# A two-layer decoder trunk on one core: products of 512 columns read their moving tile from two halves in turns

## The chip, the core and the metric

The kernel runs on one core of a Trainium2 chip, as one launch. The time is the device time of that core in microseconds. The kernel before took 1157.42 us, the median of three runs (1157.29, 1157.42 and 1157.46 us). A core has an engine for matrix products (PE, with a separate track PEld for loading the stationary operand), two elementwise engines (DVE and ACT), a third one (POOL), a queue engine (SP), and 16 DMA engines.

## The reference

A batch of one sequence of 512 tokens with 1024 features passes through two layers. Layer 0 mixes tokens with a convolution module, layer 1 with sparse attention. Each mixer is followed by a SwiGLU block. Cut to what is multiplied:

```python
D_MODEL, SEQ, DEPTH, D_FF = 1024, 512, 2, 2816
def swiglu_ffn(h, w_in, w_out):
    gate, up = jnp.split(h @ w_in, 2, axis=-1)
    return (jax.nn.silu(gate) * up) @ w_out
# layer 0:  h = rmsnorm(x, g);  x += silu(layernorm(causal_depthwise_conv(glu(h @ w_in)))) @ w_out
# layer 1:  h = rmsnorm(x, g);  q, k, v, gates = split(h @ w_in);  x += (gated compressed + selected + window attention) @ w_out
# both:     h = rmsnorm(x, g);  x += swiglu_ffn(h, w_in, w_out)
```

Everything is float32. The kernel takes each float32 operand apart into a high part, rounded to the type float32r, and a low part, the rest, also float32r, and adds three products: high times high, high times low, low times high.

## The kernel before, in words

**Layout.** Features lie on the 128 partitions, tokens along the free axis. The residual stream is eight tiles `x[0..7]` of 128 features by 512 tokens. A product of 512 columns loads a 128 by 128 block of weights as the stationary operand and reads a tile of 128 by 512 tokens as the moving one; it writes one bank of PSUM with 512 float32 columns, one per token.

**The products of 512 columns.** `mm3` (lines 320 to 323) issues the three products of one block: `wh` with `xh`, `wh` with `xl`, `wl` with `xh`. It is called from `proj_start` (line 395; the first four output tiles of a projection, k by k, with the first k written out by hand), `proj_tile` (line 424; one output tile, 8 k-steps, 24 products), `reg_tile` in the SwiGLU block (line 1117), the loop over 12 output tiles in the attention projections (line 1814) and `row_mm` (line 1191; 14 rows of the second SwiGLU matrix, each with 8 output tiles). The convolution's start (lines 499 to 513) writes its products out by hand. In the profile these products are named `pp<-hh,wh`, `pp<-hl,wh`, `pp<-a,wh`, `pp<-oh,wh`, `st<-row,wh`, `st<-ah,wh` and so on: output, then the moving tile and the weights.

**Other products.** The rest of both SwiGLU blocks goes through `product` (line 1013): block products of 256 columns (`st<-ball,sh`, `st<-ball,wh`), whose moving operand is `ball`. The attention's value projections (`v_mm`, line 1844) use slices of `hh` and `hl` as the stationary operand and 304 or 256 columns of weights as the moving one. Scores, transposes, value products and sums of squares have shapes of their own.

**Who writes the moving tiles.** `split_x` (line 347) makes `hh` and `hl` from `x`: ACT scales and rounds into `hh`, DVE writes scaled `x` minus `hh` into `hl`. It serves the convolution's input, both SwiGLU inputs and the attention's input (the columns `V_NM0`, `V_NF0`, `V_NF1`, `V_NM1` of the gains); `split_last` (line 884) does the same for the eighth tile of a SwiGLU block. `ln_mul` and `ln_low` (lines 808 to 820) make the tile `a` of the convolution's output projection, in two ACT activations and a DVE subtraction. `divide` (line 895) and `row_part` (line 1159) take the SwiGLU products `ys` apart for the row stage. `out_parts` (line 2019) makes `oh` and `ol` from the attention's output.

**Who reads the results.** In the attention, `gain` and `square` (lines 1489 and 1505) copy a projection tile out of PSUM on ACT, `v_cmp` (line 1764) multiplies two others into the tile `kr` on DVE, and lines 2137 to 2146 add the output projection to `x` on DVE. The SwiGLU and convolution stages multiply or add the PSUM tile on DVE.

**Order.** Weights arrive through a list `units` in program order: `w_dma` loads a 128 by 1024 tile on SP's queue, `w_hi` rounds it on ACT, `w_lo` subtracts on DVE, `next_w` (line 271) hands it over and starts the one after. Many instructions are pinned to program order (`held`, `pe`, `order`, `hold`), and the hooks of `proj_start`, the tables `BESIDE`, `V_BESIDE` and `FILL` and the dictionaries `ROW_AT`, `RAW_AT`, `SUM_AT` say beside which product each elementwise step is issued. The rest is ordered by the framework's scheduler. Each instruction is recorded at line 153, the helper that passes it on, so the profile is read by tile names.

Of the kernel before, what the change touches and what calls it, by code (L numbers as in the profile page):

```python
# [14 lines left out]
AF = mybir.ActivationFunctionType  # L15
ALU = mybir.AluOpType
# [3 lines left out]
P = 128  # L20
T = 512
D = 1024
NK = 8
# [12 lines left out]
V_NM0, V_NF0, V_NM1, V_NF1 = 0, 8, 16, 24  # L36
# [129 lines left out]
def trunk(ctx: ExitStack, tc: tile.TileContext, A, out):  # L166
# [71 lines left out]
    def held(ins):  # L238
        return tc.keep_in_program_order(ins) if hold[0] else ins
# [69 lines left out]
    def v(col, n=1):  # L309
        return vec[:, col:col + n]  # L310
# [6 lines left out]
    nc.gpsimd.memset(halfpi, math.pi / 2)  # L317


    def mm3(ps, wh, wl, xh, xl, first, last):  # L320
        held(nc.tensor.matmul(ps, wh, xh, start=first, stop=False))
        held(nc.tensor.matmul(ps, wh, xl, start=False, stop=False))
        held(nc.tensor.matmul(ps, wl, xh, start=False, stop=last))

    def rsqrt(pool, a, rows, n, tag):

# [20 lines left out]
    def split_x(m, gcol):  # L347
        hh[m] = hps[0].tile([P, T], F32R, tag=f"hh{m}", name=nm(f"hh{m}"))
        hl[m] = hps[0].tile([P, T], F32R, tag=f"hl{m}", name=nm(f"hl{m}"))
        g = v(gcol + m)  # L350
        held(nc.scalar.activation(hh[m], x[m], AF.Copy, scale=g))
        held(nc.vector.scalar_tensor_tensor(hl[m], x[m], g, hh[m], ALU.mult, ALU.subtract))

    def sum_x(m, acc, eng=None, on_v=False):
        sq = acc if m == 0 else tp.tile([P, T], F32, tag="sq", name=nm("sq"))
# [39 lines left out]
    def proj_start(pool, tag, xh, xl, hooks=None, pre=None, into=None):  # L395

        hooks = hooks or {}
        pss = [] if into is None else into
        pss.extend(pool.tile([P, T], F32, tag=tag, name=nm("pp")) for _ in range(4))
        if pre:  # L400
            pre(0)
        for i in range(4):
            wh, wl = next_w()
            for k2 in range(2):
                k = 2 * i + k2
                if pre and k + 1 < NK:
                    pre(k + 1)
                if k == 0 and pre:
                    for w, z in ((wh, xh), (wl, xh), (wh, xl)):
                        for m in range(4):  # L410
                            held(nc.tensor.matmul(pss[m], w[:, m * P:(m + 1) * P], z[0], start=w is wh and z is xh,
                                                  stop=False))
                for m in range(4 if k or not pre else 0):
                    c = slice(k2 * T + m * P, k2 * T + (m + 1) * P)
                    mm3(pss[m], wh[:, c], wl[:, c], xh[k], xl[k], k == 0, k == NK - 1)
                    if (k, m) in hooks:
                        hooks[k, m]()
                if k2 == 0:
                    w_lo()
                if k in hooks:  # L420
                    hooks[k]()
        return pss
# [15 lines left out]
    def conv_module():  # L438
        acc = new_acc()
        with ExitStack() as cx:  # L440
# [53 lines left out]
            for k in range(NK):  # L494
                if k < NK - 1:
                    split_x(k, V_NM0)
                if k == NK - 2:
                    split_x(NK - 1, V_NM0)
                if k == 0:
                    wh, wl = first_w()  # L500
                elif k % 2 == 0:
                    wh, wl = next_w(False)
                if k == 0:
                    load_tables()
                    for w, z in ((wh, hh), (wl, hh), (wh, hl)):
                        for m in range(2):
                            held(nc.tensor.matmul(pend[m], w[:, m * P:(m + 1) * P], z[0], start=w is wh and z is hh,
                                                  stop=False))
                    continue
                for m in range(2):  # L510
                    c = slice(k % 2 * 256 + m * P, k % 2 * 256 + (m + 1) * P)
                    for w, z in ((wh, hh), (wl, hh), (wh, hl)):
                        held(nc.tensor.matmul(pend[m], w[:, c], z[k], start=False, stop=z is hl and k == NK - 1))
            for k in range(NK):
                if k == 3:
                    w_hi(state["next"])
# [291 lines left out]
            def ln_mul(i):  # L808
                pe(nc.vector.tensor_tensor(vch[i], vch[i], rs, ALU.mult))
                lny[i] = ct.tile([P, T], F32, tag="A", bufs=3, name=f"lny{i}")  # L810
                if i == 0:
                    box["a"] = [cp.tile([P, NK * T + A_ASIDE], F32R, tag="bd", bufs=BAND_BUFS, name=f"a{s}")
                                [:, A_ASIDE:].rearrange("p (k t) -> p k t", k=NK) for s in range(2)]
                ah.append(box["a"][0][:, i, :])
                for z in (ah[i], lny[i]):
                    pe(nc.scalar.activation(z, vch[i], AF.Silu, scale=v(V_LNG + i), bias=v(V_LNB + i)))

            def ln_low(i):
                al.append(box["a"][1][:, i, :])
# [30 lines left out]
    def ffn(acc, gnext, layer, between=None):  # L850
# [9 lines left out]
        def pe(ins):  # L860
            return ins if order[0] else tc.keep_in_program_order(ins)

        with ExitStack() as cx:
# [20 lines left out]
            def split_last(part):  # L884
                m, g = NK - 1, v(gcol + NK - 1)
                if part == 0:
                    hh[m] = hps[0].tile([P, T], F32R, tag=f"hh{m}", name=nm(f"hh{m}"))
                    hl[m] = hps[0].tile([P, T], F32R, tag=f"hl{m}", name=nm(f"hl{m}"))
                    nc.scalar.activation(hh[m], x[m], AF.Copy, scale=g)
                else:  # L890
                    nc.vector.scalar_tensor_tensor(hl[m], x[m], g, hh[m], ALU.mult, ALU.subtract)

            ah, al, ys = {}, {}, {}

            def divide(f, pool):
                ah[f] = pool.tile([P, T], F32R, tag=f"ah{f}", name=nm("ah"))
                al[f] = pool.tile([P, T], F32R, tag=f"al{f}", name=nm("al"))
                held(nc.scalar.activation(ah[f], ys[f], AF.Copy))
                held(nc.vector.tensor_tensor(al[f], ys[f], ah[f], ALU.subtract))

            def new_y(f):
                k = f - EARLY - 1
# [256 lines left out]
            def row_part(f):  # L1159
                if f in ROW_SLOT:  # L1160
                    t = sw.tile([P, 2 * T], F32R, tag=ROW_SLOT[f], name=nm("row"))
                    rh[f] = h_, l_ = t[:, :T], t[:, T:]
                else:
                    rh[f] = h_, l_ = [sw.tile([P, T], F32R, tag="gc" + e, name=nm("row")) for e in "hl"]
                pe(nc.scalar.activation(h_, ys[f], AF.Copy))
                pe(nc.vector.tensor_tensor(l_, ys[f], h_, ALU.subtract))

            def block(c, d, e, neg=False):
                h_, l_ = bh[c][:, d], bl[c][:, d]
# [194 lines left out]
    def nsa(acc, cosT, sinT, gnext):  # L1364
# [124 lines left out]
        def gain(e, ps):  # L1489

            if e < 2:
                q = ap_.tile([P, T], F32, tag=f"kr{e}", name=nm("kraw"))
            elif e < 6:
                q = tp.tile([P, T], F32, tag=("sq", "sq", "acc", "Rb")[e - 2], name=nm("kraw"), bufs=2 if e < 4 else 1)
            else:
                q = op.tile([P, T], F32, tag=f"o{e - 6}", name=nm("qraw"))
            (ks if e < 6 else oT).append(q)
            raw.append(q)
            nc.scalar.activation(q, ps, AF.Copy, scale=v(V_KG + e // 2 if e < 6 else V_QG))
            rot = rots[e] = C["rots"][e % 2]  # L1500
            for b in (0, 64):
                nc.sync.dma_start(rot[b:b + 8], q[b + 8:b + 16])
                nc.sync.dma_start(rot[b + 8:b + 16], q[b:b + 8])

        def square(e, ps):
            sqs[e] = (qk.tile([P, T], F32, tag="q2", name=nm("qsq"), bufs=Q2B) if e in (4, 5) else
                      kp.tile([P, T], F32, tag="qsq", name=nm("qsq"), bufs=SQB))
            nc.scalar.activation(sqs[e], ps, AF.Square)

        def first_out():  # L1510
            gain(0, firsts[0])
# [26 lines left out]
        def to_cmp(c, a):  # L1538
            return kr[c][:, :, a, :].rearrange("p q n -> p n q")
# [10 lines left out]
        def seq16(t):  # L1550
            return t.rearrange("p (n q) -> p n q", q=16)
# [124 lines left out]
        def pe(ins):  # L1676
            return ins if order[0] else tc.keep_in_program_order(ins)
# [85 lines left out]

        def v_cmp():
            for a in range(2):
                nc.vector.tensor_tensor(to_cmp(1, a), seq16(pss[2 + a]), seq16(R), ALU.mult)
            cmp_move(1)

        extra["vc"] = v_cmp
# [364 lines left out]
        with ExitStack() as cxo:  # L2134
            po = pool(cxo, "apo", 8, space=PSUM, **rw)
            acc = new_acc()
            for m in range(NK):
                ps = proj_tile(po, "po", oh, ol)
                pin.clear()
                order[0] = m == NK - 1  # L2140
                nc.vector.tensor_tensor(x[m], x[m], ps, ALU.add)
                if m < NK - 1:
                    finish_x(m, gnext, acc, fin(m))
                else:
                    sum_x(m, acc, fin(m))
                order[0] = False
# [184 lines left out]
```

## Time and profile before

| | |
|---|---|
| median of three runs | 1157.42 us |
| profiled execution, first to last instruction (span) | 1156.3 us |
| outside the span, from these two | 1.1 us |
| granted TensorE clock, mean | 1.000 |
| PE busy | 1151.0 us, 8341 products |
| PEld busy | 1011.6 us, 8341 loads |
| DVE busy | 867.4 us, 1558 instructions |
| ACT busy | 585.1 us, 1118 instructions |
| POOL busy | 402.6 us, 441 instructions |
| DMA | 164.27 MB, mean 142 GB/s |

Busy time of PE is the union of modelled durations: the end of a product is modelled, and neighbours overlap in the record. How long a product really keeps PE is read from the distance between the starts of neighbours. A group's row gives, behind the bar, the busy time and the mean duration of one, and then the idle time of the engine ahead of it.

### The profile page before, as it was taken

The page shows a single profiled execution, that of the slowest core. Times are in us where ns is not written, and L with a number is a line of the kernel's source. Part 1 is how long each engine was busy: PE and PEld are TensorE (multiplying, and loading weights), DVE is VectorE, ACT ScalarE, POOL GpSimd, SP SyncE. Part 2 cuts the span into 40 slices and gives each one's busy share as a digit, 9 for nine tenths or more (in the row PEclk, how much of TensorE's full clock was granted, in tenths as well). Part 3 has the DMA queues.
Part 4 walks back from the last instruction along what each step waited for, and adds up shares of the span by engine and source line. Part 5 has one row for each costly group of instructions (what it writes and reads, how often), then busy time and mean ns, then how long its engine had stood idle before and what let it go on. Part 6 is the DMA issues. An engine that isn't in the chain of part 4 may idle for free.

```text
span 1156.3 us, 21728 instructions
## 1 busy us (share of the span) xinstructions
PE 1151.0 (100%) x8341; PEld 1011.6 (87%) x8341; DVE 867.4 (75%) x1558; ACT 585.1 (51%) x1118; POOL 402.6 (35%) x441
## 2 busy tenths in 40 slices
PE   9999999999999999999999999999999999999998
PEld 7888788899999988998778877778889999998898
DVE  7898786998777568875676778764699877756566
ACT  6312464565555444454333688763455555544443
POOL 1029122054444101333233577752304444430031
PEclk9999999999999999999999999999999999999999
DMA  9744428278777532534364232112736877762352
GB/s 372 268 124 125 98 91 218 92 195 200 198 192 192 155 119 92 153 104 106 110 160 113 63 75 55 38 38 91 200 109 162 205 198 190 194 184 92 109 128 73
DMA packets 86552, 164.27 MB, mean 142 GB/s; under 512 B 36656, under 2 KB 37808, under 8 KB 85680
## 3 DMA queue, kind: packets, MB, share of 16 engines
q1 hardware_dynamic: 66800, 108.48, 30.9%
q0 software_dynamic: 19504, 54.37, 20.1%
q8 instruction: 65, 1.06, 0.4%
q14 instruction: 39, 0.32, 0.1%
q10 hardware_dynamic: 144, 0.04, 0.0%
HBM read 147.23 MB, written 5.28 MB: 132 GB/s over the span
## 4 chain that ended last, share of the span: by engine, by line
PE 96%; DVE 2%; issue 1%; DMA 1%; ACT 0%; SPq 0%; DVEq 0%; ACTq 0%
PE st L153 50%; PE pp L153 29%; PE O L153 4%; PE S L153 3%; PE T L153 3%; PE pv L153 2%; PE cpe L153 1%; DVE cv L153 1%; PE warm L153 1%; PE psc L153 1%; DVE u L153 0%; DMA swap<-u 0%; PE z L153 0%; PE psq L153 0%; PE rbc L153 0%
## 5 line engine op out<-in xcount | busy, mean ns | idle before, releaser
L153 PE MATMUL st<-ball,sh 128*128 128x256 f32 x1760 | 304.9, 276 | 0.0
L153 PEld LDWEIGHTS st<-ball,sh 128*128 128x128 f32 x1760 | 265.4, 188 | 1.3 <-ACT c L153 1.0
L153 PE MATMUL st<-ball,sl 128*128 128x256 f32 x880 | 242.5, 276 | 0.0
L153 DVE TENSOR_TENSOR wl<-wr,wh 128x1024 fp32r<-128x1024 f32 (+4 forms) x145 | 179.9, 1240 | 83.3 <-ACT wh L153 83.2
L153 ACT ACTIVATE wh<-wr 128x1024 fp32r<-128x1024 f32 (+4 forms) x144 | 148.6, 1032 | 169.0 <-PE st L153 60.2
L153 POOL DMA_DIRECT2D S<-fw_x x88 | 78.3, 890 | 277.0 <-DVE sl L153 221.2
L153 POOL TENSOR_TENSOR S<-S,wr 128x512 f32<-128x512 f32 x84 | 118.2, 1407 | 147.6 <-DMA wr<-fw_op 119.3
L153 PEld LDWEIGHTS st<-ball,sl 128*128 128x128 f32 x880 | 165.3, 188 | 0.0
L153 PE MATMUL pp<-hh,wh 128*128 128x512 f32 x384 | 153.2, 399 | 0.1
L153 PE MATMUL pp<-hh,wl 128*128 128x512 f32 x384 | 149.9, 391 | 0.0
L153 PE MATMUL pp<-hl,wh 128*128 128x512 f32 x384 | 149.6, 390 | 0.0
L153 DVE TENSOR_TENSOR sl<-S,sh 128x512 fp32r<-128x512 f32 x176 | 117.9, 710 | 30.0 <-ACT sh L153 29.1
L153 PE MATMUL st<-ball,wh 128*128 128x256 f32 x704 | 124.1, 276 | 0.0
L153 ACT ACTIVATE sh<-S 128x512 fp32r<-128x512 f32 x176 | 101.0, 621 | 18.5 <-PE st L153 15.0
L153 PE MATMUL st<-row,wh 128*128 128x512 f32 x352 | 108.5, 389 | 0.0
L153 PEld LDWEIGHTS st<-ball,wh 128*128 128x128 f32 x704 | 106.4, 188 | 0.3
L153 PE MATMUL st<-ball,wl 128*128 128x256 f32 x352 | 97.0, 276 | 0.0
L153 PEld LDWEIGHTS pp<-hh,wh 128*128 128x128 f32 x384 | 72.5, 189 | 17.2 <-issue 1.9
L153 POOL TENSOR_SCALAR Pm<-Pm,mx,gates 128x512 f32<-128x512 f32 (+2 forms) x112 | 70.9, 645 | 44.3 <-DVE mx L153 23.2
L153 PEld LDWEIGHTS pp<-hh,wl 128*128 128x128 f32 x384 | 72.4, 189 | 15.5
L153 PEld LDWEIGHTS pp<-hl,wh 128*128 128x128 f32 x384 | 72.2, 188 | 14.5 <-issue 0.2
L153 ACT ACTIVATE c<-st 128x256 f32<-128x256 f32 x132 | 48.6, 377 | 65.2 <-PE st L153 48.7
(267 smaller groups left out, 2173.2 us busy)
## 6 DMA issues: line engine op xcount, KB each, us to landing
S<-fw_x POOLq DMA_DIRECT2D x88, 512.0 KB, 5.9
wr<-fw_in SPq DMA_DIRECT2D x44, 512.0 KB
wr<-fw_or SPq DMA_DIRECT2D x28, 512.0 KB
r<-fw_x SPq DMA_DIRECT2D x44, 256.0 KB
bd<-bands POOLq DMA_DIRECT2D x6, 1280.0 KB, 17.5
wr<-cw_in SPq DMA_DIRECT2D x14, 512.0 KB
wr<-fw_s SPq DMA_DIRECT2D x8, 512.0 KB
wr<-fw_op SPq DMA_DIRECT2D x8, 512.0 KB
```

The source lines that it names most:

```text
L153: z = f(*a, **kw)
```

## The change

Every product of 512 float32r columns goes through a new helper, `wide_mm`. It reads the moving tile in another order: first column 0, then column 256, then 1, then 257, and so on, so that two runs of 256 columns (1024 bytes apart on each partition) are read in turns. Output columns are written one after another as before: output column 2n is the product of stored column n, output column 2n + 1 that of stored column n + 256.

So that the results come out in the order of the tokens, most moving tiles are now stored with the even tokens in the first half and the odd ones in the second: the source is read with a step of two elements (`parted_tokens`) and the tile is written as two runs (`stored`). This holds for `hh` and `hl` of the convolution and of both SwiGLU blocks, for the tile `a` and its companion `lny`, and for the row stage's `ah`, `al` and `row`.

Two tiles stay in token order: `hh` and `hl` of the attention, which `v_mm` also uses as stationary slices, and `oh` and `ol`. There the PSUM tile comes out in turns (token n at column 2n, token n + 256 at column 2n + 1), and the readers sort it out: `gain`, `square`, `v_cmp` and the last addition to `x` read PSUM with a step of two.

Products of 256 columns, value projections, scores and all others are as before. The number of instructions is the same.

```diff
+    def woven(z):
+        return z.rearrange("p (a n) -> p n a", a=2)
+    def stored(z):
+        return z.rearrange("p (a n) -> p a n", a=2)
+    def parted_tokens(z):
+        return z.rearrange("p (n a) -> p a n", a=2)
+    def wide_mm(ps, w, z, first, last):
+        held(nc.tensor.matmul(ps.rearrange("p (n a) -> p n a", a=2), w, woven(z), start=first, stop=last))
     def mm3(ps, wh, wl, xh, xl, first, last):
-        held(nc.tensor.matmul(ps, wh, xh, start=first, stop=False))
-        held(nc.tensor.matmul(ps, wh, xl, start=False, stop=False))
-        held(nc.tensor.matmul(ps, wl, xh, start=False, stop=last))
+        wide_mm(ps, wh, xh, first, False)
+        wide_mm(ps, wh, xl, False, False)
+        wide_mm(ps, wl, xh, False, last)
...
         g = v(gcol + m)
-        held(nc.scalar.activation(hh[m], x[m], AF.Copy, scale=g))
-        held(nc.vector.scalar_tensor_tensor(hl[m], x[m], g, hh[m], ALU.mult, ALU.subtract))
+        z, h_, l_ = x[m], hh[m], hl[m]
+        if gcol != V_NM1:
+            z, h_, l_ = parted_tokens(z), stored(h_), stored(l_)
+        held(nc.scalar.activation(h_, z, AF.Copy, scale=g))
+        held(nc.vector.scalar_tensor_tensor(l_, z, g, h_, ALU.mult, ALU.subtract))
...
                 for z in (ah[i], lny[i]):
-                    pe(nc.scalar.activation(z, vch[i], AF.Silu, scale=v(V_LNG + i), bias=v(V_LNB + i)))
+                    pe(nc.scalar.activation(stored(z), parted_tokens(vch[i]), AF.Silu, scale=v(V_LNG + i),
+                                            bias=v(V_LNB + i)))
...
-                held(nc.scalar.activation(ah[f], ys[f], AF.Copy))
-                held(nc.vector.tensor_tensor(al[f], ys[f], ah[f], ALU.subtract))
+                held(nc.scalar.activation(stored(ah[f]), parted_tokens(ys[f]), AF.Copy))
+                held(nc.vector.tensor_tensor(stored(al[f]), parted_tokens(ys[f]), stored(ah[f]), ALU.subtract))
...
-                pe(nc.scalar.activation(h_, ys[f], AF.Copy))
-                pe(nc.vector.tensor_tensor(l_, ys[f], h_, ALU.subtract))
+                pe(nc.scalar.activation(stored(h_), parted_tokens(ys[f]), AF.Copy))
+                pe(nc.vector.tensor_tensor(stored(l_), parted_tokens(ys[f]), stored(h_), ALU.subtract))
...
-            nc.scalar.activation(q, ps, AF.Copy, scale=v(V_KG + e // 2 if e < 6 else V_QG))
+            nc.scalar.activation(stored(q), parted_tokens(ps), AF.Copy, scale=v(V_KG + e // 2 if e < 6 else V_QG))
...
-            nc.scalar.activation(sqs[e], ps, AF.Square)
+            nc.scalar.activation(stored(sqs[e]), parted_tokens(ps), AF.Square)
...
-                nc.vector.tensor_tensor(to_cmp(1, a), seq16(pss[2 + a]), seq16(R), ALU.mult)
+                nc.vector.tensor_tensor(to_cmp(1, a).rearrange("p (b m) q -> p b m q", b=2),
+                                        pss[2 + a].rearrange("p (m q b) -> p b m q", q=16, b=2),
+                                        R.rearrange("p (b m q) -> p b m q", b=2, q=16), ALU.mult)
...
-                nc.vector.tensor_tensor(x[m], x[m], ps, ALU.add)
+                nc.vector.tensor_tensor(stored(x[m]), stored(x[m]), parted_tokens(ps), ALU.add)
```

The products written out by hand in the convolution's start and in `proj_start` become calls of `wide_mm` with the same operands, and `split_last` changes as `split_x` does.

More of the change, by code (lines that the diff above doesn't have):

```diff
@@ L410, in proj_start @@
                         for m in range(4):
-                            held(nc.tensor.matmul(pss[m], w[:, m * P:(m + 1) * P], z[0], start=w is wh and z is xh,
-                                                  stop=False))
+                            wide_mm(pss[m], w[:, m * P:(m + 1) * P], z[0], w is wh and z is xh, False)
                 for m in range(4 if k or not pre else 0):
@@ L506, in conv_module @@
                         for m in range(2):
-                            held(nc.tensor.matmul(pend[m], w[:, m * P:(m + 1) * P], z[0], start=w is wh and z is hh,
-                                                  stop=False))
+                            wide_mm(pend[m], w[:, m * P:(m + 1) * P], z[0], w is wh and z is hh, False)
                     continue
@@ L512, in conv_module @@
                     for w, z in ((wh, hh), (wl, hh), (wh, hl)):
-                        held(nc.tensor.matmul(pend[m], w[:, c], z[k], start=False, stop=z is hl and k == NK - 1))
+                        wide_mm(pend[m], w[:, c], z[k], False, z is hl and k == NK - 1)
             for k in range(NK):
@@ L888, in split_last @@
                     hl[m] = hps[0].tile([P, T], F32R, tag=f"hl{m}", name=nm(f"hl{m}"))
-                    nc.scalar.activation(hh[m], x[m], AF.Copy, scale=g)
+                    nc.scalar.activation(stored(hh[m]), parted_tokens(x[m]), AF.Copy, scale=g)
                 else:
-                    nc.vector.scalar_tensor_tensor(hl[m], x[m], g, hh[m], ALU.mult, ALU.subtract)
+                    nc.vector.scalar_tensor_tensor(stored(hl[m]), parted_tokens(x[m]), g, stored(hh[m]), ALU.mult,
+                                                   ALU.subtract)
             ah, al, ys = {}, {}, {}
```

## The prediction

> **What bounds the kernel now.** I looked first at the cores and the PE row of the page, then at PE's waits, then at the starts of neighbouring products in the timeline, last at the chain of waits.
>
> ```profile
> core 0: 1156.3 us, clock 1.000
> PE 1151.0 (100%) x8341; PEld 1011.6 (87%) x8341; DVE 867.4 (75%) x1558; ACT 585.1 (51%) x1118; POOL 402.6 (35%) x441
> PE warm L153 <- DVE zb L153: 1.0, 1, 1.0
> PE cpe L153 <- DMA uf<-swap: 0.4, 1, 0.4
> PE lnpt L153 <- DVE red L153: 0.4, 1, 0.4
> ```
>
> PE is busy all the time at a full clock, and its recorded waits come to 1.8 us of 1156.3. But this busy time is the union of modelled durations that overlap, so it can't say whether PE runs at its best rate. The starts can:
>
> ```profile
> 839.77 0.39 PE L153 MATMUL pp<-hl,wh 128*128 128x512 f32 x1
> ...
> 841.81 0.39 PE L153 MATMUL pp<-hl,wh 128*128 128x512 f32 x1
> ```
>
> These are the first and the last of ten neighbours: nine distances in 2.04 us, 226.7 ns for a product of 512 float32r columns (not the 390 ns of its modelled duration). The chain of waits gives the same over long stretches, and beside it the rate of another type:
>
> ```profile
> 135.79 1.73 PE warm L153 x8
> 137.51 46.50 PE pp L153 x204
> ...
> 188.58 38.12 PE pp L153 x168
> ...
> 776.68 43.76 PE pp L153 x192
> ```
>
> 38.12 / 168 is 226.9 ns, 43.76 / 192 is 227.9, 46.50 / 204 is 227.9: hardly anything but the products' own rate lies in these stretches. The `warm` products also have 512 columns, but bfloat16 (128 zeros read four times), and take 1.73 / 8 = 216.2 ns. So a float32r product loses 10.5 ns against them, 4.9%. Is that a fixed part per instruction, or a loss per column? The products of 256 columns answer:
>
> ```profile
> 899.78 0.28 PE L153 MATMUL st<-ball,wh 128*128 128x256 f32 x1
> ...
> 904.77 0.39 PE L153 MATMUL st<-ball,wh 128*128 128x256 f32 x2
> ```
>
> Between these two starts lie 44 distances (each row of the pattern is one or two products, three in 0.34 us): 4.99 / 44 = 113.4 ns, half of 226.7 to the tenth. A fixed part would show as more than half. The loss goes with the columns that are read. The stream of the moving operand is therefore what sets the pace, and it is just its order that the change alters.
>
> **How many products are altered.**
>
> ```profile
> 0.00:1157.00 1157.00, 358.39 (x1536) 287.16 (x1536) 34.10 (x50) 17.46 (x28) 1.00 0.51 142
> 0.00:1157.00 1157.00, 120.01 (x528) 99.18 (x528) 14.89 (x22) 13.33 (x22) 1.00 0.51 142
> 0.00:1157.00 1157.00, 30.28 (x96) 18.03 (x96) 8.93 (x6) 3.75 (x6) 1.00 0.51 142
> 0.00:1157.00 1157.00, 18.73 (x48) 9.02 (x48) 8.93 (x6) 1.00 0.51 142
> ```
>
> This is the view by stretches over the whole span, for the tiles `pp`, `row`, `ah` and `al` in turn (first count: products on PE). 1536 + 528 + 96 + 48 = 2208 products, at 226.7 ns 500.6 us, 43% of the span. The other 6133 aren't touched.
>
> **The change part by part.** *The stream.* The trace has no moving operand that jumps between two places from column to column, so its price must be bounded. Below stands the bfloat16 row: 216.2 ns, a gain of 10.5 ns each. Above stands the dearest product of 512 columns that the trace shows:
>
> ```profile
> 121.86 0.59 PE L153 MATMUL lnst<-u,onesb 128*32 128x512 f32 x1
> ...
> 122.29 0.59 PE L153 MATMUL lnst<-u,onesb 128*32 128x512 f32 x1
> ```
>
> Plain float32, 0.43 us from start to start, 203 ns more than now. These bounds are far apart. I take the lower one, since it is the row nearest in distance (5% against 90%), in the kind of loss and in what is read: a stream that runs forward through memory loses a little per column, steadily, which looks like a pause each time the reader moves on to a new piece; with two streams in turns the move in one can be made while the other is read. That is an argument and not a measurement, hence the second rival.
>
> [...]
>
> *Where the gain counts.* Where PE is the bound, all of it. Two stretches are bound elsewhere; first the stages as a whole (PE, PEld, DVE, ACT, POOL, clock, DMA share), then `pp` alone in those two:
>
> ```profile
> 5.00:27.00 22.00, 22.00 (x104) 18.35 (x103) 18.95 (x34) 13.43 (x20) 3.93 (x7) 1.00 1.02 405
> 27.00:73.00 46.00, 46.00 (x204) 37.91 (x202) 41.20 (x52) 13.78 (x16) 0.00 (x0) 1.00 0.66 233
> 95.00:112.00 17.00, 17.00 (x232) 14.19 (x226) 16.61 (x21) 3.62 (x5) 17.00 (x14) 1.00 0.62 159
> 184.00:227.00 43.00, 43.00 (x202) 35.92 (x201) 38.95 (x63) 21.20 (x31) 3.64 (x3) 1.00 0.56 155
> 397.00:475.00 78.00, 78.00 (x354) 64.90 (x353) 53.07 (x81) 32.54 (x49) 7.12 (x7) 1.00 0.35 106
> 4.00:27.00 23.00, 20.83 (x86) 16.61 (x87) 0.00 (x0) 0.00 (x0) 1.00 1.02 403
> 82.00:112.00 30.00, 22.66 (x96) 17.96 (x96) 1.28 (x2) 0.00 (x0) 1.00 0.44 114
> ```
>
> From 5 to 27 us the DMA engines are full (share 1.02): the 86 products there wait for weights and `x`, and I count no gain. From 82 to 112 us DVE is busy 16.61 of 17 us in the part shown: the 96 products there don't count either. Elsewhere DVE has room even after the gain: from 27 to 73 us PE would fall by 204 x 10.5 ns = 2.1 us to 43.9, DVE needs 41.20; from 184 to 227 by 2.1 to 40.9, DVE needs 38.95; the row stage has 53.07 against 78. If a faster PE met DVE's order there, the two tight stages would give back up to 2.1 us each.
>
> *The steps of two.* Reads with a step of two replace contiguous ones on ACT and DVE; writes stay in runs. Their nearest rows:
>
> ```profile
> L153 DVE TENSOR_TENSOR gr<-pp,Rb 128x512 f32<-128x512 f32 x8 | 5.5, 686 | 1.8 <-ACT Rb L153 1.5 <-PE pp L153 0.3
> L153 DVE TENSOR_TENSOR kr<-pp,Rb 128x512 f32<-128x512 f32 x2 | 2.1, 1110 | 3.0 <-PE pp L153 3.0
> L153 DVE TENSOR_REDUCE red<-lng 128x64 f32<-128x512 f32 x1 | 0.7, 692 | 1.0 <-PE lng L153 1.0
> L153 ACT ACTIVATE rows<-lnst 128x512 f32<-128x512 f32 x1 | 0.6, 579 | 0.0
> L153 ACT ACTIVATE qa<-psq 128x512 f32<-128x512 f32 x3 | 1.8, 599 | 4.8 <-PE psq L153 4.8
> ```
>
> `red` reads PSUM with a step of 64 elements and `rows` with a step of 8: 692 and 579 ns, as much as the contiguous 686 and 599. `kr` is *written* with a step and costs 424 ns more than `gr`. So I take zero for a read, and 0.42 us as its upper bound. What covers it: the steps of the SwiGLU inputs, the row stage (11 `row` parts of a layer, 4.7 us at the bound, against 25 us of room on DVE) and the attention's copies lie beside PE. Without cover stand the convolution's first eight `hl` steps, at most 8 x 0.42 = 3.4 us. `v_cmp` already writes with a step. No DMA, no queue and no wait is moved or added.
>
> *The sum.* 2208 - 86 - 96 = 2026 products x 10.5 ns = 21.3 us. The profiled execution's span of 1156.3 us becomes 1135.0; with the 1.1 us between it and the median of 1157.4, 1136.1 us.
>
> **The rivals.** *Half a cure.* Each stream still pauses, but every other pause is hidden: 5.2 ns each, 2026 x 5.2 = 10.5 us, 1147 us. The exact half at 256 columns says that the loss is one small thing that repeats, and nothing says that two streams hide all of it.
>
> *The line is fetched anew at each column: slower.* The price sits in every one of the 2208 products. It decides as soon as a distance goes above 226.7 ns. At the plain float32 row's 430 ns it is 2208 x 203 ns = 449 us, 1606 us; a mild form, as large a loss again as today's (10.5 ns), gives 2208 x 10.5 = 23 us, 1180 us. For it: 226.7 ns shows that a reader in order doesn't get its data for nothing. Against it: a forward stream changes pieces too, and pays only 10.5 ns in 512 columns for all its changes.
>
> *The loss is one of amount, not of order.* If four bytes per column can simply not be delivered faster, the change does nothing on PE: 1157 us, up to 1161 with the 3.4 us of the first steps. For it: the loss is strictly in proportion. Against it: a limit of amount would have to sit just 4.9% under the bfloat16 rate, though a float32r column has twice the bytes.
>
> **How the numbers follow.** About 0.2%, 2.3 us, is what a measurement can tell from no change. Full cure 0.50 (1136), half 0.14 (1147), nothing 0.10 (1157 to 1161), new line per column 0.26, of which 0.06 mild (up to 1180). The range begins at 1128: all 2208 products gain (23.2 us), and the distance falls by a further 2.8 ns each (6.2 us), since nothing here proves that the bfloat16 row is a floor. It ends at 1180 and so leaves out the 0.20 of the dear form. Faster 0.64, the two cures. Within 0.2%: 0.08, most of the third rival; slower: 0.28, the rest of it and the second. As both signs have weight: the forecast's own range is 1128 to 1142.
>
> **What would show each step.** Ten neighbours of `pp` start 216 ns apart instead of 226.7, and those of 256 columns stay at 113.4; the chain's piece of 168 `pp` is 36.3 us long. The stretches before 27 us and from 82 to 112 us keep their length. `hl<-x` and `row<-y` on DVE keep their mean. The forecast is wrong if the distance is 227 or more; if it is 216 and the span is still over 1145 us, the gain was lost to DVE's order.

## The result, and the profile after

| | before | after |
|---|---|---|
| median, us | 1157.44 (four runs, 1157.29 to 1158.19) | 1140.56 (four runs, 1139.92 to 1141.59) |
| span of the profiled execution, us | 1156.3 | 1138.9 |
| PE busy, us | 1151.0 | 1128.8 |
| DVE busy, us | 867.4 | 870.7 |
| ACT busy, us | 585.1 | 598.0 |

The ratio is 0.9855, with a 95% interval from 0.9841 to 0.9869. The change makes the kernel faster by 16.9 us. That is 1.4%. The forecast was 1136.1 us, 21.3 us faster.

First the cores, the PE row of the page and the longest of PE's waits (in total, times, longest), all of the kernel after:

```profile
core 0: 1138.9 us, clock 1.000
PE 1128.8 (99%) x8341; PEld 1012.7 (89%) x8341; DVE 870.7 (76%) x1558; ACT 598.0 (53%) x1118; POOL 402.3 (35%) x441
PE bc L153 <- DVE kcb L153: 1.3, 1, 1.3
PE cpe L153 <- issue: 0.8, 1, 0.8
PE st L153 <- DVE t L153: 0.8, 2, 0.4
PE pp L153 <- DVE wl L153: 0.6, 3, 0.3
PE pp L153 <- DVE a L153: 0.5, 1, 0.5
```

PE is still the busy engine, at the same full clock and with the same number of products. But its list of waits, which held three entries before, now has DVE in it many times. And ACT is busy 12.9 us longer, though no instruction was added. Both points come back below.

Then the starts of neighbouring products in the timeline after, first and last of eight `pp`:

```profile
830.92 0.38 PE L153 MATMUL pp<-hh,wh 128*128 128x512 f32 x1
...
832.43 0.38 PE L153 MATMUL pp<-hl,wh 128*128 128x512 f32 x1
```

Seven distances in 1.51 us are 215.7 ns each, where there were 226.7. The products do run at the rate that was forecast.

Now the chain of waits, where the long pieces of `pp` are, first before and then after:

```profile
5.44 16.90 PE pp L153 x72
...
26.91 46.28 PE pp L153 x204
73.19 9.48 PE cpe L153 x320
...
828.11 38.12 PE pp L153 x168
```

```profile
27.30 44.03 PE pp L153 x204
71.34 8.66 PE cpe L153 x290
...
82.94 10.36 PE pp L153 x48
...
99.12 10.56 PE pp L153 x48
...
814.82 5.20 PE pp L153 x24
...
821.67 1.41 DVE z L153 x2
823.08 1.14 DVE wl L153
...
836.21 15.38 PE pp L153 x70
```

44.03 / 204 and 10.36 / 48 are 215.8 ns again. Taken together, the rows tell three things. The first long piece begins 0.39 us *later* than before, so the start of the kernel lost more than its gain. The 96 products between 82 and 112 us are links of the chain (before, the chain ran over DVE there, mostly `cv`), and the table below has them gain in full. And the piece of 168 products near 828 us, which was one unbroken link before, is now cut up: DVE's `z`, `ball` and `wl` stand between a piece of 24 and one of 70.

The order of the instructions on PE is the same in both kernels but for one pair of neighbours, so the start of each product can be compared with its own start before. The table is worked out from these starts. "Gain due" is the number of altered products in the stage times 10.9 ns; "lost" is what of it didn't arrive (a minus sign: more arrived). The last column is the same for the kernel `sort_psum`, told below.

| stage, by times before, us | altered products | gain due | kernel ahead at its end | lost | lost in `sort_psum` |
|---|---|---|---|---|---|
| start, to 26.98 | 85 | 0.93 | -0.38 | 1.31 | 0.17 |
| first projection, to 73.22 | 203 | 2.21 | 1.85 | -0.02 | -0.02 |
| `cpe`, to 83.13 | 0 | 0 | 0.78 | 1.07 | 0.90 |
| convolution, to 115.04 | 96 | 1.05 | 1.89 | -0.06 | -0.07 |
| layer norm, to 137.75 | 1 | 0.01 | 2.52 | -0.62 | -0.53 |
| its output projection, to 184.10 | 203 | 2.21 | 3.47 | 1.26 | 0.53 |
| SwiGLU inputs, to 226.76 | 180 | 1.96 | 5.00 | 0.43 | 0.43 |
| block products, to 397.19 | 0 | 0 | 4.13 | 0.87 | 0.56 |
| row stage, to 474.81 | 336 | 3.66 | 7.81 | -0.02 | -0.02 |
| attention inputs, to 549.72 | 153 | 1.67 | 9.57 | -0.09 | -0.09 |
| projections, to 615.08 | 222 | 2.42 | 10.52 | 1.47 | 1.15 |
| scores and values, to 776.95 | 10 | 0.11 | 10.88 | -0.25 | -0.02 |
| output and SwiGLU inputs, to 866.29 | 383 | 4.17 | 14.63 | 0.42 | 0.42 |
| block products, to 1036.08 | 0 | 0 | 13.75 | 0.88 | 0.60 |
| row stage, to 1114.71 | 335 | 3.65 | 17.42 | -0.02 | -0.02 |

In all 24.1 us were due (2208 x 10.9 ns), 17.4 arrived, and 6.7 were lost.

Some rows of the table change from one execution to the next. A second profile of the changed kernel (`changed_again`, below) lost 2.01 us at the start. A second one of `sort_psum` lost 0.36 at `cpe` instead of 0.90, and then won nothing back in the layer norm. The start hangs on when PE gets to its full pace: in the profile after, the `warm` products go from 427 to 217 ns apart at 3.9 us, while before and in `changed_again` all of them are 427 ns apart.

### The profile page after: what moved, and what is told of

Its sections match the earlier page's. It is cut to its first block, busy times and chain, and to the rows that moved or that the text cites. A ratio compares the mean times of both kernels' runs of the same rounds, so it can differ in the third digit from the quotient of the medians.

```text
span 1138.9 us, 21740 instructions
## 1 busy us (share of the span) xinstructions
PE 1128.8 (99%) x8341; PEld 1012.7 (89%) x8341; DVE 870.7 (76%) x1558; ACT 598.0 (53%) x1118; POOL 402.3 (35%) x441
## 4 chain that ended last, share of the span: by engine, by line
PE 88%; DVE 6%; ACT 2%; issue 2%; DMA 1%; POOL 1%; SPq 0%; DVEq 0%; POOLq 0%; ACTq 0%
PE st L153 48%; PE pp L153 22%; PE O L153 4%; PE S L153 3%; PE T L153 3%; PE cpe L153 3%; PE pv L153 2%; DVE z L153 1%; DVE wl L153 1%; DVE c L153 1%; PE psc L153 1%; ACT hh L153 0%; DMA x<-xT 0%; ACT ball L153 0%; ACT wh L153 0%
## 5 line engine op out<-in xcount | busy, mean ns | idle before, releaser
L153 DVE TENSOR_TENSOR wl<-wr,wh 128x1024 fp32r<-128x1024 f32 (+4 forms) x145 | 176.4, 1217 | 69.7 <-ACT wh L153 69.4
L153 PE MATMUL pp<-hh,wh 128*128 128x512 f32 x384 | 148.0, 386 | 0.5 <-ACT hh L153 0.3
L153 PE MATMUL pp<-hh,wl 128*128 128x512 f32 x384 | 146.0, 381 | 0.7 <-DVE wl L153 0.6
L153 PE MATMUL pp<-hl,wh 128*128 128x512 f32 x384 | 145.6, 380 | 0.2 <-DVE hl L153 0.2
L153 PE MATMUL st<-row,wh 128*128 128x512 f32 x352 | 104.7, 379 | 0.0
L153 PEld LDWEIGHTS pp<-hl,wh 128*128 128x128 f32 x384 | 72.5, 189 | 10.9 <-DVE hl L153 1.1
## 6 DMA issues: line engine op xcount, KB each, us to landing
bd<-bands POOLq DMA_DIRECT2D x6, 1280.0 KB, 16.9
```

The costliest lines, as they stand in the source:

```text
L153: z = f(*a, **kw)
```

## The experiments

They ask two questions. Why is a moving tile read faster in two streams than in order? And where did the 6.7 us go?

**Fourteen orders of reading (`orders`).** The row stage has 14 rows of 24 products in each layer. Each row of the kernel before is read in an order of its own. The results come out in other places, so this run serves for the distances alone. The diff is shortened to the patterns of the moving tile:

```diff
-                    mm3(pss[m], wh[:, c], wl[:, c], *rh[RROWS[j]], j == 0, j == NR - 1)
+                        vo, vz = ordered(ORDERS[(j + 7 * layer) % NR], pss[m], z)
+                        held(nc.tensor.matmul(vo, w[:, c], vz, start=..., stop=...))
+    streams of n:       z "p (a n) -> p n a"
+    near, l apart:      z "p (b a n) -> p b n a"
+    step of n:          z "p (n a) -> p a n"
+    runs of l by turns: z "p (a n l) -> p n a l"
```

> The kernel before, with 14 reading orders of the moving tile in the row stages, one for each of the 14 rows (24 products each), in the second layer shifted by seven rows; the values of the outputs are permuted, so this run is for the distances alone. Theory A, two streams hide the move of the reader from piece to piece, and a piece has 16 columns (226.7 ns against 216 is one pause in 16 columns): in order 226.7 ns; 2, 4 and 8 streams far apart 216; two streams 64 or 16 columns apart 216; 8 or 4 columns apart about 227, since both streams then lie in the same piece most of the time; runs of 16 from each half in turns 227, runs of 2, 4 and 8 216; a step of two 237 and a step of four 257, with two and four times as many moves. Rival B, it is being exactly consecutive that costs: every order but the first takes 216. [...]

The timeline gives the first product of each row, so the distance is a difference of two starts by 24:

```profile
402.47 0.38 PE L156 MATMUL st<-ah,wh 128*128 128x512 f32 x1
...
407.65 0.45 PE L156 MATMUL st<-ah,wh 128*128 128x512 f32 x1
...
414.44 0.68 PE L156 MATMUL st<-row,wh 128*128 128x512 f32 x1
...
426.11 0.42 PE L156 MATMUL st<-row,wh 128*128 128x512 f32 x1
...
446.87 0.62 PE L156 MATMUL st<-row,wh 128*128 128x512 f32 x1
...
457.68 0.64 PE L156 MATMUL st<-row,wh 128*128 128x512 f32 x1
...
468.75 0.51 PE L156 MATMUL st<-row,wh 128*128 128x512 f32 x1
```

The row of two streams takes from 402.47 to 407.65: 5.18 / 24 is 215.8 ns. Four streams (407.65 to 414.44) take 282.9, eight (to 426.11) 486.3. A step of two (446.87 to 457.68) takes 450.4, a step of four (to 468.75) 461.3. All the rows, the same in both layers within 4 ns and the runs of two within 6:

| order | ns |
|---|---|
| in order | 228 to 229 |
| two streams, 256 apart | 215.8 |
| two streams, 64 / 16 / 8 / 4 apart | 217.5 / 215.8 / 215.8 / 215.8 |
| four streams, eight streams | 282.8, 486.5 |
| step of two, step of four | 450 to 454, 461 |
| runs of 2 / 4 / 8 / 16 from each half in turns | 334 to 340 / 250 / 243 / 240 |

Two streams only four columns apart cure the loss as well as two that lie 256 apart (215.8 ns both). So the idea that one piece of memory is fetched while another is read, with the halves far apart, isn't needed. Theory A had expected 227 ns for streams 8 or 4 columns apart, and rival B 216 for every order but the first: both fall. And more streams make it worse: the loss that the prediction's second rival expected doesn't come with two streams, but one does come with four (282.8 ns) and eight (486.5).

**Fourteen more (`orders_2`).** These numbers suggested theory D in the text below. It is the author's guess at a cause; no trace shows the pairs and pieces that it speaks of. What the run can decide is whether the distances that it expects come. The same edit with other orders, among them each column twice in a row, and one column 512 times (shortened as above):

```diff
+    halves, step s:     z "p (a n s) -> p s n a"
+    near, l apart:      z "p (b a n) -> p b n a"
+    each column twice:  z[:, :256].unsqueeze(2).to_broadcast([128, 256, 2])
+    one column:         z[:, :1].to_broadcast([128, 512])
+    short:              the first 128 columns in order; the first 256 in two streams
```

> The kernel before with 14 more ways to read the moving tile in the row stages, one per row, in the second layer shifted by four rows; outputs are wrong and some ways read only part of the tile: this run is for distances alone. After the first list (two streams 216 ns at any distance from 4 to 256 columns; four streams 283; steps of two and four 450 and 461; runs of 2, 4, 8, 16 from each half 334, 250, 243, 240) theory A with its piece of 16 columns has fallen. Theory D: columns are fetched in pairs, the even and the odd one each from a piece of four columns of its own; four fetches in turn from one piece cost nothing (two streams), two a little (in order), one double (steps). Rival E: the two fetches of a pair get in each other's way when they fall in the same piece. They differ here: two halves, each read with a step of two: D 227, E 216. Each column read twice in a row: D 216, E 227 or more. Two halves with a step of four: D 450. A step of eight 461 by both; two streams two columns apart 227 by both; one column read 512 times: D 216. Four streams 4, 16 and 64 columns apart and eight 4 apart: by D above 227, how far is open. In order 227, two streams 216, as before. Products of 128 columns show the pace of the weight load alone, 107 to 112 ns; products of 256 as two streams show whether it holds them: the same number if so, 108 if not.

```profile
403.42 0.39 PE L156 MATMUL st<-ah,wh 128*128 128x512 f32 x1
...
408.86 0.38 PE L156 MATMUL st<-ah,wh 128*128 128x512 f32 x1
...
414.04 0.40 PE L156 MATMUL st<-row,wh 128*128 128x512 f32 x1
...
419.50 0.61 PE L156 MATMUL st<-row,wh 128*128 128x512 f32 x1
...
430.36 0.40 PE L156 MATMUL st<-row,wh 128*128 128x512 f32 x1
...
435.58 0.59 PE L156 MATMUL st<-row,wh 128*128 128x512 f32 x1
...
445.91 0.24 PE L156 MATMUL st<-row,wh 128*128 128x128 f32 x1
...
448.55 0.48 PE L156 MATMUL st<-row,wh 128*128 128x512 f32 x1
```

In turn: two streams from the halves, each with a step of two (403.42 to 408.86), 226.7 ns; each column twice, 215.8; two streams two columns apart, 227.5; halves with a step of four, 452.5; one column 512 times, 217.5; a step of eight, 430.4; and products of 128 columns, 110.0. From the rows that aren't quoted: four streams 4, 16 and 64 columns apart take 270, 269 and 283 ns, eight streams 479, products of 256 columns in two streams 112.5.

Two rows decide. *Each column twice* is a single forward stream, and it is cured (215.8 ns): two streams aren't what helps. *The halves with a step of two* are two streams 1024 bytes apart, and they aren't cured (226.7). Theory D had expected 216 and 227 for these two before the run, and rival E the reverse. Most of the distances for 512 columns lie in three groups: 215.8 to 217.5 ns (two streams four or more columns apart, each column twice, one column), 226.7 to 229 (in order, two streams two columns apart, the halves with a step of two) and 450 to 461 (steps of two and four, the halves with a step of four). Four streams (269 to 283), eight (479 to 486.5), the runs by turns (240 to 340) and a step of eight (430, where 461 was expected) lie in none. Theory D got most of the distances right; what causes them isn't shown.

**The sorting alone (`sort_alone`).** Everything of the change, but the products read their tiles in order:

```diff
-        held(nc.tensor.matmul(ps.rearrange("p (n a) -> p n a", a=2), w, woven(z), start=first, stop=last))
+        held(nc.tensor.matmul(ps, w, z, start=first, stop=last))
```

> Everything of the change but the two streams: the tiles are stored and read out with their steps of two, the products read in order (so tokens come out permuted). Theory: the distance is 226.7 ns again, ACT and DVE pay their 150 to 250 ns as in the changed kernel, but with the slower PE almost all of it is covered; what is not covered is the first stage, +1 to 2 us: 1158 to 1160 us. Rival: the steps cost 5 us on the path whatever PE does: 1162 us.

The median is 1157.3 us, beside 1157.3 for the kernel before on that chip: a ratio of 1.0001 (0.9991 to 1.001). So as long as PE reads in order the steps of two cost nothing that the interval of about 1.1 us either way would show, and the whole gain is the order of reading. The 1158 to 1160 us that were expected didn't come, because ACT and DVE didn't pay the 150 to 250 ns that were assumed (below).

**Sorted where the results are read (`sort_psum`, `sort_psum_2`).** Here all moving tiles stay in token order, and ACT and DVE make them with contiguous reads and writes. PE still reads them in two streams, and the readers of PSUM sort, as the attention's do in the changed kernel:

```diff
-            z, h_, l_ = parted_tokens(z), stored(h_), stored(l_)
...
-                pe(nc.vector.tensor_tensor(gr, pG, R, ALU.mult))
+                pe(nc.vector.tensor_tensor(stored(gr), parted_tokens(pG), stored(R), ALU.mult))
...
-                pe(nc.scalar.activation(stored(h_), parted_tokens(ys[f]), AF.Copy))
-                pe(nc.vector.tensor_tensor(stored(l_), parted_tokens(ys[f]), stored(h_), ALU.subtract))
+                pe(nc.scalar.activation(h_, ys[f], AF.Copy))
+                pe(nc.vector.tensor_tensor(l_, ys[f], h_, ALU.subtract))
...
-                pe(nc.vector.tensor_tensor(x[m], x[m], pss[m], ALU.add))
+                pe(nc.vector.tensor_tensor(stored(x[m]), stored(x[m]), parted_tokens(pss[m]), ALU.add))
```

> All moving tiles stay in token order, read as two streams; the order is put right where DVE and ACT read PSUM. Theory: 10.9 ns x 2208 = 24.1 us are gained on PE, and some 3 to 5 us of the 7 us that are given back come from reads of SBUF with a step of two (ACT 614 to 863 ns, DVE 684 to 839); reads of PSUM with that step cost nothing (690 to 689, 687 to 685). Then this takes 1135 to 1138 us, row<-y goes back to 614 and 684 ns, gr and ar stay at 686. Rival: what is given back is DVE's order and waits that a faster PE meets anyway, whatever the reads cost: 1140 to 1141 us. Second rival: the PSUM reads cost DVE as much as the SBUF reads did, 155 ns for each of some 64 more: 1140 us or above.

It took 1138.08 us (1137.39 to 1139.72), a ratio of 0.9836 (0.9821 to 0.9851). The interval meets that of the changed kernel, so both were run again side by side on one chip, the changed kernel as `changed_again`:

> The version sorted at PSUM once more, beside the changed kernel: 1138 us, 2 to 3 us below it; by the rival within 1 us.

> The changed kernel once more, on the same chip as the version sorted at PSUM: 1140 to 1141 us. If reads of SBUF with a step of two are what costs it the difference, it stays 2 to 3 us above that version; the rival, that the two were only measured on different chips, has them within 1 us.

`sort_psum_2` 1138.08 us (1137.74 to 1138.8), `changed_again` 1140.77 (1140.44 to 1142.25). The runs don't overlap: the steps of two on SBUF cost 2.7 us in the changed kernel. The chain of waits of `sort_psum` shows where the largest part of it was:

```profile
5.44 16.34 PE pp L153 x72
...
26.16 44.03 PE pp L153 x204
```

The 72 products of the start are one link of 16.34 us, and the long piece begins at 26.16, not at 27.30: 1.14 us of the 2.7. In the changed kernel they waited for ACT and DVE. By `changed_again`, whose early pace is like that of `sort_psum`, the start's share is larger: 2.01 - 0.17, or 1.8 us.

The four kernels make a square: PE reads in order or in two streams, and ACT and DVE read `y` contiguously or with a step of two. The row of the groups for the same two instructions, in the order before (in order, contiguous), `sort_alone` (in order, step of two), `sort_psum` (two streams, contiguous) and after (two streams, step of two); behind the bar, busy time in us and mean ns of one:

```profile
L153 ACT ACTIVATE row<-y 128x512 fp32r<-128x512 f32 x22 | 13.3, 614 | 0.0
L153 DVE TENSOR_TENSOR row<-y,row 128x512 fp32r<-128x512 f32 x22 | 14.9, 684 | 0.0
```

```profile
L153 ACT ACTIVATE row<-y 128x512 fp32r<-128x512 f32 x22 | 14.2, 656 | 0.0
L153 DVE TENSOR_TENSOR row<-y,row 128x512 fp32r<-128x512 f32 x22 | 14.9, 685 | 0.0
```

```profile
L153 ACT ACTIVATE row<-y 128x512 fp32r<-128x512 f32 x22 | 13.3, 613 | 0.0
L153 DVE TENSOR_TENSOR row<-y,row 128x512 fp32r<-128x512 f32 x22 | 14.9, 684 | 0.0
...
L153 DVE TENSOR_TENSOR gr<-pp,Rb 128x512 f32<-128x512 f32 x8 | 5.5, 686 | 1.3 <-ACT Rb L153 1.3
```

```profile
L153 ACT ACTIVATE row<-y 128x512 fp32r<-128x512 f32 x22 | 18.8, 863 | 0.0
L153 DVE TENSOR_TENSOR row<-y,row 128x512 fp32r<-128x512 f32 x22 | 18.3, 839 | 0.0
...
L153 ACT ACTIVATE lny<-c,vec 128x512 f32<-128x512 f32 x6 | 6.3, 1055 | 0.0
L153 ACT ACTIVATE qraw<-pp,vec 128x512 f32<-128x512 f32 x8 | 5.5, 689 | 24.1 <-PE pp L153 24.1
```

Neither the two streams nor the step of two is dear by itself (614, 656 and 613 ns on ACT, 684, 685 and 684 on DVE). The two together are: 863 and 839. The trace after shows the same within one kernel, in ACT's `ah<-y`, whose reads all have a step of two there:

```profile
220.54 0.88 ACT L153 ACTIVATE ah<-y 128x512 fp32r<-128x512 f32 x1
...
244.18 0.68 ACT L153 ACTIVATE ah<-y 128x512 fp32r<-128x512 f32 x1
```

The first runs beside products in two streams, the second beside block products, whose moving operand PE reads in order; in the kernel before, these two took 616 and 632 ns. So these steps of two take longer on ACT and DVE while PE reads its two streams; no trace shows what slows them. Reads of PSUM with a step of two are free even then: `gr` in `sort_psum` stays at 686 ns, `qraw` after the change at 689 (690 before).

**The narrow products too (`narrow_too`).** If the loss goes with the columns, the 3696 products of 256 columns have it as well. This is `sort_psum` with those in two streams, their readers sorting PSUM:

```diff
-                        pe(nc.tensor.matmul(ps[:, :H], p_[:, k], m_[c][:, t], ...))
+                        pe(nc.tensor.matmul(ps[:, :H].rearrange("p (n a) -> p n a", a=2), p_[:, k], woven(m_[c][:, t]), ...))
...
-                pe(nc.scalar.activation(t, ps[:, :H], AF.Copy))
+                pe(nc.scalar.activation(stored(t), parted_tokens(ps[:, :H]), AF.Copy))
```

> As the version sorted at PSUM, and the products of 256 columns also read their moving operand as two streams of 128. If the loss is one of the stream alone, their distance goes from 113.4 to 108 ns: 3696 x 5.4 = 20 us, 1116 us. If the weight load of 128 columns is next (products of 128 columns are never closer than 107 to 109 ns), it stops at 109: 3696 x 4.4 = 16 us, 1120 us. If DVE, which is busy 135 of 170 us in these stages, or a read of PSUM is late, less. Rival: for 256 columns the weight load already sets 113.4 and nothing moves: 1136 us.

It is the fastest version: 1132.86 us (1132.28 to 1133.12), a ratio of 0.9788 (0.9774 to 0.9803), 5.2 us below `sort_psum`. The timelines, first of the kernel after (in order), then of `narrow_too`, each row of the pattern three products:

```profile
904.80 0.28 PE L153 MATMUL st<-ball,sl 128*128 128x256 f32 x1
...
907.86 0.28 PE L153 MATMUL st<-ball,sl 128*128 128x256 f32 x1
```

```profile
880.05 0.28 PE L153 MATMUL st<-ball,sl 128*128 128x256 f32 x1
...
882.73 0.28 PE L153 MATMUL st<-ball,sl 128*128 128x256 f32 x1
```

3.06 us for 27 products are 113.3 ns, 2.68 us for 24 are 111.7. The cure of the stream would give 107.9 (half of 215.8), and the 1116 to 1120 us that were expected; the loss does go with the columns, but only 1.6 of the 5.4 ns come back. The 110.0 ns of the products with 128 columns, whose stream is only half as long, are the nearest row to what may hold them up: the load of the next weights, one for each product. In the kernel before, products of only 64 columns (`psc<-kcb,qraw`) start 112 ns apart too (median). That the load is the floor is an inference from these two rows and wasn't tried by itself; nor was another order for the stationary operand.

## Why the prediction was right, and where it was off

**The bound and the rate: right, the rate in part by luck.** The bound was read from the distance of neighbours, the loss was put down to the stream of the moving operand, and the bfloat16 row was taken as what the cure would reach: 216.2 ns forecast, 215.8 measured. 10.9 ns instead of 10.5 add 0.9 us over the 2208 products.

**The reason given for the cure: wrong in its kind.** The prediction let the move in one stream be made while the other is read. Each column twice in one stream (215.8), and two streams with a step of two (226.7), rule that out. What the price hangs on instead, no trace shows. The choice of the full cure, and with it the sum, rested in part on the refuted reason. So it was in part luck that this order gained the whole 10.9 ns; the prediction had called the reason an argument and not a measurement.

**The rivals.** Half a cure, and a loss of amount, fell with the 215.8 ns. The loss at each column, the slower rival, didn't come with two streams; four and eight streams, or a step of two, did bring one (283, 486 and 450 ns).

**Where the gain counts: wrong for both exclusions, 1.9 us in the sum.** The step that failed took full DMA engines (share 1.02), and a busy DVE (16.61 of 17 us), for a bound of PE. PE's three recorded waits before lie in neither stretch. The 96 products from 82 to 112 us weren't bound by DVE: it is busy there, and the chain before ran over it, but that stage gained 1.1 us, all that was due. The 72 products from 5.44 us were one link of PE in the chain before already. The start, counted at nothing, ended 0.4 us later; `sort_psum`, where it gained 0.76 of 0.93, shows that DMA didn't hold it up, but the slower `hh` and `hl` steps did.

**The steps of two: a term that was mis-sized.** The prediction put it so: "So I take zero for a read, and 0.42 us as its upper bound." Its rows `red` and `rows` read PSUM with steps, not SBUF, and while PE read no two streams, so they couldn't show what the two do together. Measured: ACT's `row<-y` +249 ns, DVE's +155, `lny` +254 (801 before), all inside the bound; 2.7 us of the kernel's time, of which 1.1 to 1.8 at the start, as the uncovered place was named, and 0.7 (1.26 - 0.53) in the convolution's output projection, which wasn't named. The row stage, with its cover of 25 us on DVE, lost nothing, as forecast. The forecast that `hl<-x` and `row<-y` on DVE would keep their means was wrong (889 to 958 and 684 to 839 ns).

**The waits that a faster PE meets: the larger term that was mis-sized.** The sum put them at nothing; beside it, up to 2.1 us were allowed to DVE's order in each of two tight stages. The one from 27 to 73 us lost nothing, the one from 184 to 227 us 0.43, so the chain's unbroken piece of 168 products, named as a sign, didn't come. The table has 4.0 us lost in all in `sort_psum`, where the reads are contiguous: 0.56 and 0.60 in the block products, where PE waits for DVE's `t` (0.8 us in the kernel after), 0.90 at `cpe`, whose wait (0.6 us) shows no releaser, 0.53 and 0.43 and 0.42 where `a` or `wl` comes late (0.5 and 0.6 us in the kernel after), and 1.15 in the attention's projections, where `bc` waits 1.1 us for `kcb`; other stages give 0.6 back. The last isn't DVE's order: DVE itself sat idle 1.3 us before `kcb`, until POOL, which comes behind the transfer `rot<-qraw` in the chain. These places are read from the waits and the chain; none was tested by itself.

**The sum.** The 21.3 us of the forecast, with 0.9 for the better rate and 1.9 for the 182 products left out, are 24.1 us due. Less 4.0 for the waits and 2.7 for the steps of two they are 17.4 of span. So errors of both signs partly cancelled. The rest of the 4.5 us between forecast and result lies outside the span: the profiled execution after took 1140.71 us, 1.8 us more than its span, where the prediction took 1.1 by setting a span beside a median of other runs.

## What to carry to other kernels

Read PE's pace from the starts of neighbours and set it beside another type of the same shape; a steady gap of some per cent at a full clock (here 226.7 against 216.2 ns) may be cured by the order in which the moving operand is read, as it was here. For these float32r products two streams, even four columns apart, were enough (215.8 ns); more were worse (282.8 with four, 486.5 with eight). A busy engine beside PE is no bound by that alone: look for PE's waits. Where an order must be undone, try it where PSUM is read, with the SBUF tiles left contiguous for ACT and DVE: here that was 2.7 us faster than the steps of two on SBUF.

## What the hardware showed that was not expected

- The time of a float32r product of 512 columns hung on the order of its columns, and not only on the number of streams: 215.8 ns in two streams from the halves and with each column twice in one stream, 226.7 in two streams with a step of two, 228 to 229 in order, 450 to 461 with a step of two or four. No trace shows why, nor why four streams took 269 to 283 ns, the runs by turns 240 to 340 and a step of eight 430.
- With a step of two on SBUF, ACT's and DVE's `row<-y` took 207 and 154 ns longer when PE read in two streams than when it read in order (863 against 656, 839 against 685 ns).
- A float32r product of 128 columns takes 110 ns, hardly less than the 111.7 of one with 256 columns read in two streams (113.3 in order).
